# Gate products of the product-key experts: the first-index one-hots written to DRAM in one half and read back in the other

## The chip, the cores and the metric

The kernel runs on one core of one Trainium2 chip. The metric is the device time of one execution, in microseconds (us). Three runs of the kernel before gave 2181.5, 2175.8 and 2181.01 us, so its median is 2181.01 us.

## What is computed

The program is a decoder trunk of two layers over 256 positions of width 1024. Each layer has a mixer (four groups: differential attention, a convolution module, a gated convolution, a spatial gating unit) and then a product-key expert stage. Only the expert stage matters here:

```python
def peer_ffn(h, wq, keys, u_tab, v_tab):
    q = (h @ wq).reshape(b, s, PEER_HEADS, 2, PEER_HALF)
    sc = jnp.einsum('bshpd,hpnd->bshpn', q, keys)
    half_s, half_i = lax.top_k(sc, PEER_TOPK)                 # 16 of 128 keys, for each of two halves
    cand = half_s[..., 0, :, None] + half_s[..., 1, None, :]
    top_s, top_c = lax.top_k(cand.reshape(..., 256), PEER_TOPK)
    i1 = take(half_i[..., 0, :], top_c // 16)                 # first index, 0..127
    i2 = take(half_i[..., 1, :], top_c % 16)                  # second index, 0..127
    expert = i1 * 128 + i2                                    # one of 16384 single-neuron experts
    gate = jax.nn.softmax(top_s)
    act = gelu(einsum('td,thkd->thk', h, u_tab[expert]))
    return einsum('thk,thkd->td', gate * act, v_tab[expert])
```

Each of the 256 tokens picks 8 heads x 16 = 128 experts. The kernel gathers nothing: it computes the activation of all 16384 experts for all tokens, multiplies each by its gate (zero for experts not picked), and multiplies the result with the whole table v.

## The kernel before

**Stages.** In each layer, after `queries` and `topk`, two long loops stream the tables u and v through the TensorE. One step of either loop takes one 128x1024 fp32 block (512 KB) of the table. `Stream.load` (line 152) reads it into a raw tile (4 of them), `Stream.split` turns it into a rounded part `hi` (ScalarE, line 164) and a remainder `lo` (line 171, on GpSimd or on VectorE by a share: 0.8 of them on GpSimd in the stretches that matter here, 0.4 in the second half of `down`), with three buffers each, two steps ahead of use. All loads are issued by SyncE in one queue.

`up` has 128 steps, one for each value of the second index (the low part of the expert number is the partition). A step is 24 matmuls of 256 columns (lines 323 to 325) and a Gelu on ScalarE (line 845) into `acts`, four tiles of 32 steps each. `down` has 128 steps of 12 matmuls of 512 columns (line 874). A step needs the activations of its 128 experts split in two: `prep` makes the rounded part on ScalarE (line 860) and the remainder on VectorE (line 861, tile `mid`, two of them), one step ahead.

**The gates.** Between the two, `gates` scales the activations. For 8 tokens at a time (a block) it builds a one-hot of the first index, `o1` (128 picks x 8 tokens x 128 values, fp16, line 816, 128x1024), a one-hot of half of the second index, `o2` (128x512, line 819), and `og`, that one-hot times the gate, as two fp16 parts (two operations at line 823). Sixteen small matmuls (line 828) make the gate of every expert of that half for the 8 tokens in a PSUM bank. Two operations at line 834 multiply the bank into two tiles of `acts`; they are called the closing pair here. One half of the second index (`hf` 0, values 0 to 63) is done beside the second 64 steps of `up`, the other (`hf` 1, values 64 to 127) beside the first 64 steps of `down`, before the steps that use it. Each half is 32 blocks, made by two generators of 16 blocks each (even and odd blocks). `o1` does not depend on the half and is built in both, so line 816 runs 2 layers x 2 halves x 32 = 128 times.

**What sets the order.** `Background` interleaves such generators with the steps: each `yield` gives a VectorE cost, a latency and a TensorE cost, and after each step of `up` or `down` `pump(STEP)` lets as much background work in as the planned VectorE time allows, earlier generators first. `GATECOST` is (0.7, 1.2, 0.7, 0.9): `o1`, `o2` with `og`, the matmuls, the closing pair. A scheduler of the tile framework then sets the order on each engine, and may place an instruction some steps from where the code records it. After step 63 of `down` in layer 0 the same planner feeds in 40 operations of the modulation for layer 1 (line 247); the scheduler moves the first of them ahead into the steps with gates.

Of the kernel before, what the change touches and what calls it, by code (L numbers as in the profile page):

```python
# [12 lines left out]
FP16 = mybir.dt.float16  # L13
U32 = mybir.dt.uint32
AF = mybir.ActivationFunctionType
ALU = mybir.AluOpType
AX = mybir.AxisListType

P = 128
D = 1024  # L20
T = 256
# [18 lines left out]
GATECOST = (0.7, 1.2, 0.7, 0.9)  # L40
# [140 lines left out]
class Trunk:  # L181
# [618 lines left out]
            nc.vector.tensor_tensor(out=glo, in0=gv, in1=ghi, op=ALU.subtract)  # L800
            yield 1.2

    def gates(self, hf, acts, first):

        nc, one = self.nc, self.one
        half = self.iota[:, 64 * hf:64 * hf + 64]
        for t0 in range(8 * first, T, 16):  # L810
            o1 = one.tile([P, 4, P, 2], FP16, name="o1", bufs=2)
            o2 = one.tile([P, 4, 64, 2], FP16, name="o2", bufs=1)
            og = one.tile([P, 4, 2, 64, 2], FP16, name="og", bufs=2)
            i1, i2 = [self.idx[:, s, t0:t0 + 8].rearrange("p (a j) -> p a j", j=2) for s in range(2)]
            g = self.gidx[:, 2 * t0:2 * t0 + 16].rearrange("p (a j) -> p a j", j=2)
            nc.vector.tensor_tensor(out=o1, in0=self.iota[:, None].to_broadcast([P, 4, P, 2]),  # L816
                                    in1=i1[:, :, None].to_broadcast([P, 4, P, 2]), op=ALU.is_equal)
            yield GATECOST[0], 0.3
            nc.vector.tensor_tensor(out=o2, in0=half[:, None].to_broadcast([P, 4, 64, 2]),  # L819
                                    in1=i2[:, :, None].to_broadcast([P, 4, 64, 2]), op=ALU.is_equal)  # L820
            for s in range(2):
                gs = g.rearrange("p (a s) j -> p a s j", s=2)[:, :, s]
                nc.vector.tensor_tensor(out=og[:, :, s], in0=o2, in1=gs[:, :, None].to_broadcast([P, 4, 64, 2]), op=ALU.mult)  # L823
            yield GATECOST[1], 0.3
            b = self.accs(1)[0] if hf == 0 else self.bank()
            for j in range(8):
                for s in range(2):
                    nc.tensor.matmul(b[:, 64 * j:64 * j + 64], o1[:, j // 2, :, j % 2], og[:, j // 2, s, :, j % 2],  # L828
                                     start=s == 0, stop=s == 1)
            yield 0.0, 0.5, GATECOST[2]  # L830
            b = b.rearrange("p (j c) -> p c j", j=8)
            for s, act in enumerate(acts):
                a = act[:, :, t0:t0 + 8]
                nc.vector.scalar_tensor_tensor(out=a, in0=b[:, 32 * s:32 * s + 32], scalar=1.0 / GSCALE, in1=a,  # L834
                                               op0=ALU.mult, op1=ALU.mult)
            yield GATECOST[3]
# [48 lines left out]
    def experts(self, l, area):  # L885
        nc = self.nc
        sc, hb = self.queries(l, area)

        def picks():
            yield from self.topk(sc, area)  # L890
            if l + 1 < L:
                area.reset()
                cr = self.cond(area)
                bufs = [area.take(D + 1) for _ in range(4)]
                yield from self.mod_tiles(l, list(range(40, 48)), cr, bufs, pace=PACE[0])
                yield from self.mod_tiles(l + 1, list(range(8)), cr, bufs, pace=PACE[0])

        self.bg.add(picks())
        acts = [self.big(32, T) for _ in range(2)]
        self.stream.pool_share = SHARE[0]  # L900
        run = self.up(hb, acts)
        next(run)
        self.stream.pool_share = SHARE[1]
        acts += [self.big(32, T) for _ in range(2)]
        for i in range(2):
            self.bg.add(self.gates(0, acts[0:2], i))
        next(run)
        self.bg.finish()
        for i in range(2):
            self.bg.add(self.gates(1, acts[2:4], i))  # L910
        self.stream.pool_share = SHARE[2]
        run = self.down(acts)
        next(run)
        self.stream.pool_share = SHARE[3]
        self.m = Carve(self.big(), self.big())
        if l + 1 < L:
            cr = self.cond(self.m)
            bufs = [self.m.take(D + 1) for _ in range(4)]
            self.bg.add(self.mod_tiles(l + 1, list(range(8, 48)), cr, bufs, pace=PACE[1]))
            self.m.reset()  # L920
        next(run)
        self.bg.finish()
        self.m2 = Carve(self.big())
        if l + 1 < L:
            self.params(l + 1)
            self.bias = self.m.take(4, 256)
        y = self.m2.take(2, D)
        for tt in range(2):
            for d in range(2):
                eng = nc.vector.tensor_copy if d else nc.scalar.copy  # L930
                eng(out=y[:, tt, 512 * d:512 * d + 512], in_=self.acc[2 * tt + d])
        for c in range(NC):
            b = self.bank()
            for tt in range(2):
                nc.tensor.transpose(out=b[:, P * tt:P * tt + P], in_=y[:, tt, P * c:P * c + P], identity=self.ident)
            nc.vector.scalar_tensor_tensor(out=self.xT[:, c], in0=b[:, 0:T], scalar=self.modT[:, l, 40 + c:41 + c],
                                           in1=self.xT[:, c], op0=ALU.mult, op1=ALU.add)
            if l + 1 == L:
                self.last_stats(c, NC if c == NC - 1 else c - 2)
# [191 lines left out]
```

## Time and profile before

| | |
|---|---|
| median of three runs | 2181.01 us (2175.8 to 2181.5) |
| the profiled execution's own time | 2180.3 us |
| its span, first to last instruction | 2178.4 us |
| TensorE matmuls busy | 1932.3 us (89% of the span) |
| VectorE busy | 1673.4 us (77%) |
| GpSimd busy | 1277.4 us (59%) |
| ScalarE busy | 951.2 us (44%) |
| read from HBM | 371.9 MB, written 1.6 MB |

The profiled execution lies 0.7 us under the median; 1.9 us of it lie outside the span. In the profile PE is the TensorE's matmuls and PEld its weight loads, DVE is VectorE, ACT ScalarE, POOL GpSimd, SP SyncE. A line number is that of the kernel. Tile names are shown without their buffer numbers, so `o1` and `o2` are both `o`, told apart by their size. The arrow reads "out<-in". A trace answer for a stretch gives busy time inside it and the number of instructions; the granted clock of the TensorE is a share of full speed.

### The profile page before, as it was taken

Reading aid. Unit: us, or ns where it says so; the run is one execution under the profiler, and the core shown is the slowest. Engines: PE = TensorE matmul, PEld = TensorE weight load, DVE = VectorE, ACT = ScalarE, POOL = GpSimd, SP = SyncE. Lnnn points to the kernel's source line nnn. Section 1 sums busy time; section 2 is a strip of 40 time slices with the busy share of each in tenths; the row PEclk is TensorE's granted clock in tenths of the full one; section 3 lists DMA queues with packets and bytes.
Section 4 is the critical chain, followed back from the end, with each engine's and each line's share of the span. In section 5 each row is a group of like instructions: output and inputs, shape, how many; then the busy total and the mean of one; then the engine's idle time right before and its main releaser. Section 6 shows DMA issues by size and latency. Waiting matters only on the chain. (4 is left out here: it accounts for less than half of the span.)

```text
span 2178.4 us, 35318 instructions
## 1 busy us (share of the span) xinstructions
PE 1932.3 (89%) x13718; PEld 1736.7 (80%) x13718; DVE 1673.4 (77%) x2739; ACT 951.2 (44%) x1441; POOL 1277.4 (59%) x518
## 2 busy tenths in 40 slices
PE   4767997999999888899994889999999998889998
PEld 3667997998999666677874779999999976768886
DVE  6997699768892999987556676997598778884555
ACT  4344442443344333345552554444343443335554
POOL 6535676984566554543347657899565655545333
PEclk7888998999999998999997999999999999999999
DMA  7555445754455446687651444556444554446663
GB/s 263 197 187 175 159 161 186 249 175 136 141 169 175 136 130 210 248 283 264 194 184 58 136 136 140 182 164 186 153 156 152 168 155 130 138 132 191 194 193 116
DMA packets 104522, 375.82 MB, mean 173 GB/s; under 512 B 11900, under 2 KB 13217, under 8 KB 104098
## 3 DMA queue, kind: packets, MB, share of 16 engines
q1 hardware_dynamic: 104354, 373.57, 52.6%
q8 instruction: 107, 1.75, 0.3%
q14 instruction: 61, 0.50, 0.1%
HBM read 371.94 MB, written 1.58 MB: 171 GB/s over the span
## 5 line engine op out<-in xcount | busy, mean ns | idle before, releaser
L171 POOL TENSOR_TENSOR lo<-raw,hi 128x1024 fp32r<-128x1024 f32 x473 | 1234.4, 2617 | 858.2 <-ACT hi L164 836.0
L164 ACT ACTIVATE hi<-raw 128x1024 fp32r<-128x1024 f32 x600 | 635.5, 1060 | 643.7 <-issue 374.0
L325 PE MATMUL bank<-mid,lo 128*128 128x256 f32 x2432 | 700.8, 288 | 47.8 <-POOL lo L171 46.8
L323 PE MATMUL bank<-mid,hi 128*128 128x256 f32 x2432 | 707.9, 292 | 25.3 <-ACT hi L164 11.5
L324 PE MATMUL bank<-mid,hi 128*128 128x256 f32 x2432 | 700.1, 288 | 18.4 <-DVE mid L313 9.2
L874 PE MATMUL acc<-hi,mid 128*128 128x512 f32 x2048 | 585.8, 404 | 63.6 <-DVE mid L861 62.8
L325 PEld LDWEIGHTS bank<-mid,lo 128*128 128x128 f32 x2432 | 477.3, 196 | 52.3 <-POOL lo L171 51.1
L874 PEld LDWEIGHTS acc<-hi,mid 128*128 128x128 f32 x2048 | 390.9, 195 | 159.7 <-DVE mid L861 79.2
L323 PEld LDWEIGHTS bank<-mid,hi 128*128 128x128 f32 x2432 | 478.0, 197 | 31.2 <-ACT hi L164 13.5
L324 PEld LDWEIGHTS bank<-mid,hi 128*128 128x128 f32 x2432 | 478.1, 197 | 20.5 <-DVE mid L313 10.9
L861 DVE TENSOR_TENSOR mid<-big,mid 128x256 fp32r<-128x256 f32 x256 | 201.9, 793 | 197.1 <-PE acc L874 174.8
L874 PE MATMUL acc<-lo,mid 128*128 128x512 f32 x1024 | 327.1, 401 | 1.2 <-DVE lo L171 1.0
L860 ACT ACTIVATE mid<-big 128x256 fp32r<-128x256 f32 x256 | 107.0, 418 | 434.0 <-PE acc L874 426.4
L874 PEld LDWEIGHTS acc<-lo,mid 128*128 128x128 f32 x1024 | 198.0, 194 | 45.2 <-DVE lo L171 1.6
L171 DVE TENSOR_TENSOR lo<-raw,hi 128x1024 fp32r<-128x1024 f32 x127 | 159.5, 1256 | 82.1 <-ACT hi L164 81.3
L247 DVE SCALAR_TENSOR_TENSOR big<-big 128x1025 f32<-128x1025 f32 x96 | 175.3, 1841 | 17.5 <-DMA big<-wmod 17.5
L816 DVE TENSOR_TENSOR o<-iota,idx 128x1024 f16<-128x1024 f16 x128 | 187.0, 1462 | 0.0
L823 DVE TENSOR_TENSOR og<-o,gidx 128x512 f16<-128x512 f16 x256 | 181.7, 747 | 1.1
L819 DVE TENSOR_TENSOR o<-iota,idx 128x512 f16<-128x512 f16 x128 | 145.9, 1140 | 2.9
L828 PEld LDWEIGHTS <-o 128*128 128x128 f16 x2048 | 69.8, 99 | 41.3 <-issue 25.3
L845 ACT ACTIVATE big<-bank 128x256 f32<-128x256 f32 x256 | 93.5, 365 | 0.0
L834 DVE SCALAR_TENSOR_TENSOR big<-acc,big 128x256 f32<-128x256 f32 x128 | 47.8, 414 | 38.8 <-PE acc L828 38.8
(200 smaller groups left out, 1569.9 us busy)
## 6 DMA issues: line engine op xcount, KB each, us to landing
raw<-u SPq DMA_DIRECT2D x256, 512.0 KB, 3.5
raw<-v SPq DMA_DIRECT2D x256, 512.0 KB, 3.6
big<-wmod SPq DMA_DIRECT2D x96, 512.5 KB, 5.0
raw<-win SPq DMA_DIRECT2D x40, 512.0 KB, 3.5
raw<-wq SPq DMA_DIRECT2D x32, 512.0 KB, 3.5
raw<-wout SPq DMA_DIRECT2D x16, 512.0 KB, 3.5
big<-keys SPq DMA_DIRECT2D x2, 1024.0 KB, 6.1
xT<-xT SPq DMA_DIRECT2D x2, 512.0 KB, 4.3
```

Source lines behind the costliest of these rows:

```text
L164: nc.scalar.activation(out=hi, in_=raw, func=AF.Copy)
L171: eng.tensor_tensor(out=lo, in0=raw, in1=hi.bitcast(F32), op=ALU.subtract)
L247: nc.vector.scalar_tensor_tensor(out=w, in0=w, scalar=1.0, in1=sc, op0=ALU.mult, op1=ALU.mult, accum_out=self.modT[:, l, j:j + 1])
L323: mm(out, whi, hhi, start=start, stop=False)
L324: mm(out, whi, hlo, start=False, stop=False)
L325: mm(out, wlo, hhi, start=False, stop=stop)
L816: nc.vector.tensor_tensor(out=o1, in0=self.iota[:, None].to_broadcast([P, 4, P, 2]), in1=i1[:, :, None].to_broadcast([P, 4, P, 2]), op=ALU ...
L819: nc.vector.tensor_tensor(out=o2, in0=half[:, None].to_broadcast([P, 4, 64, 2]), in1=i2[:, :, None].to_broadcast([P, 4, 64, 2]), op=ALU.is ...
L823: nc.vector.tensor_tensor(out=og[:, :, s], in0=o2, in1=gs[:, :, None].to_broadcast([P, 4, 64, 2]), op=ALU.mult)
L860: nc.scalar.activation(out=a[:, 0], in_=src, func=AF.Copy)
L861: nc.vector.tensor_tensor(out=a[:, 1], in0=src, in1=a[:, 0].bitcast(F32), op=ALU.subtract)
L874: nc.tensor.matmul(self.acc[2 * tt + d], a[:, s, P * tt:P * tt + P], w[:, 512 * d:512 * d + 512], start=i == 0 and s == 0 and w is whi, st ...
```

## The change

The one-hots `o1` of half 0 are written to DRAM tiles (`kept`, 32 for each layer, 256 KB each) as they are made. In half 1 they are not built again. Each is read back: the first one when its generator starts, the next one as soon as the matmuls of the present block are recorded. `o1` has three buffers where it had two. Since half 1 has no operation at line 816, its `yield` (0.7 planned VectorE cost and 0.3 latency) is not passed there either.

```diff
-    def gates(self, hf, acts, first):
+    def gates(self, hf, acts, first, kept):
         nc, one = self.nc, self.one
         half = self.iota[:, 64 * hf:64 * hf + 64]
+        def onehot(t0):
+            return one.tile([P, 4, P, 2], FP16, name="o1", bufs=3)
+
+        def fetch(t0):
+            o1 = onehot(t0)
+            nc.sync.dma_start(out=o1, in_=kept[t0 // 8])
+            return o1
+
+        o1 = fetch(8 * first) if hf else None
         for t0 in range(8 * first, T, 16):
-            o1 = one.tile([P, 4, P, 2], FP16, name="o1", bufs=2)
+            if not hf:
+                o1 = onehot(t0)
             o2 = one.tile([P, 4, 64, 2], FP16, name="o2", bufs=1)
             og = one.tile([P, 4, 2, 64, 2], FP16, name="og", bufs=2)
...
-            nc.vector.tensor_tensor(out=o1, in0=self.iota[:, None].to_broadcast([P, 4, P, 2]),
-                                    in1=i1[:, :, None].to_broadcast([P, 4, P, 2]), op=ALU.is_equal)
-            yield GATECOST[0], 0.3
+            if not hf:
+                nc.vector.tensor_tensor(out=o1, in0=self.iota[:, None].to_broadcast([P, 4, P, 2]),
+                                        in1=i1[:, :, None].to_broadcast([P, 4, P, 2]), op=ALU.is_equal)
+                nc.sync.dma_start(out=kept[t0 // 8], in_=o1)
+                yield GATECOST[0], 0.3
...
                     nc.tensor.matmul(b[:, 64 * j:64 * j + 64], o1[:, j // 2, :, j % 2], og[:, j // 2, s, :, j % 2],
                                      start=s == 0, stop=s == 1)
+            if hf and t0 + 16 < T:
+                o1 = fetch(t0 + 16)
             yield 0.0, 0.5, GATECOST[2]
...
+        kept = [self.dram.tile([P, 4, P, 2], FP16, name=f"kept{l}_{i}") for i in range(T // 8)]
         for i in range(2):
-            self.bg.add(self.gates(0, acts[0:2], i))
+            self.bg.add(self.gates(0, acts[0:2], i, kept))
         next(run)
         self.bg.finish()
         for i in range(2):
-            self.bg.add(self.gates(1, acts[2:4], i))
+            self.bg.add(self.gates(1, acts[2:4], i, kept))
```

The change moves instructions as well. The first place is VectorE in the first steps of `down` in layer 0 (tiles `o_`: 128x1024 is `o1`, 128x512 is `o2`; `mid` is `prep` for one step). Before, three blocks come in four steps, and the two blocks of a pair share a step:

```order
L816 TENSOR_TENSOR o_7506<-iota,idx 128x1024
L861 TENSOR_TENSOR mid<-big,mid 128x256
L819 TENSOR_TENSOR o_7507<-iota,idx 128x512
L823 TENSOR_TENSOR og<-o_7507,gidx 128x4x128 x2
L819 TENSOR_TENSOR o_7511<-iota,idx 128x512
L861 TENSOR_TENSOR mid<-big,mid 128x256
L834 SCALAR_TENSOR_TENSOR big<-bank,big 128x32x8 x2
L816 TENSOR_TENSOR o_7510<-iota,idx 128x1024
L823 TENSOR_TENSOR og<-o_7511,gidx 128x4x128 x2
L819 TENSOR_TENSOR o_7580<-iota,idx 128x512
```

The same place with the change (line 831 is `o2`, 835 `og`, 848 the closing pair, 875 `prep`):

```order
L831 TENSOR_TENSOR o_7651<-iota,idx 128x512
L875 TENSOR_TENSOR mid<-big,mid 128x256
L848 SCALAR_TENSOR_TENSOR big<-bank,big 128x32x8 x2
L835 TENSOR_TENSOR og<-o_7651,gidx 128x4x128 x2
L171 TENSOR_TENSOR lo<-raw,hi 128x1024
L831 TENSOR_TENSOR o_7697<-iota,idx 128x512
L875 TENSOR_TENSOR mid<-big,mid 128x256
L848 SCALAR_TENSOR_TENSOR big<-bank,big 128x32x8 x2
L835 TENSOR_TENSOR og<-o_7697,gidx 128x4x128 x2
```

With the change there is exactly one block to one step, and `og` of the next block stands behind the closing pair of the block before. On the TensorE (no rows of it stand here; its order gives the counts) the 32 blocks of half 1 then end after step 33 of `down` in both layers (12 matmuls between one block and the next), where they ended after step 49 in layer 0 and after step 54 in layer 1.

The second place is SyncE's queue at the start of `down` in layer 0. Before, it holds nothing but table blocks there:

```order
L152 DMA raw<-u 128x1024 x85
L152 DMA raw<-v 128x1024 x36
```

With the change (`kept_` the DRAM tile of a block, line 815 the read):

```order
L815 DMA o_7412<-kept_0_4441 128x1024
L152 DMA raw<-u 128x1024 x2
L815 DMA o_7419<-kept_1_4442 128x1024
L152 DMA raw<-u 128x1024 x2
L815 DMA o_7463<-kept_2_4443 128x1024
L152 DMA raw<-u 128x1024 x9
L152 DMA raw<-v 128x1024 x8
L815 DMA o_7509<-kept_4_4445 128x1024
L152 DMA raw<-v 128x1024
L815 DMA o_7555<-kept_6_4447 128x1024
```

From there on a read and a table block alternate until block 31. The even blocks come first (0, 2, ... 30), then the odd ones; block 1, read at the start, keeps its buffer until the even ones are done, so these share the two others. The read that stands behind table block v[m+5] is for the matmuls behind step m+1.

## Rows read from the trace of the kernel before

**Rows 1.** Busy time of the engines in three stretches; the first row names the columns.

```profile
core 0: us, PE busy (x) PEld busy (x) DVE busy (x) ACT busy (x) POOL busy (x), PEclk, DMA share, GB/s
697.60:829.10 131.50, 113.83 (x772) 89.89 (x771) 120.72 (x176) 50.10 (x70) 62.98 (x26) 0.94 0.44 140
1542.40:1752.60 210.20, 202.13 (x2027) 200.37 (x2025) 169.62 (x204) 83.10 (x127) 125.53 (x51) 0.98 0.50 158
1752.70:1961.45 208.75, 181.47 (x1151) 142.11 (x1151) 177.75 (x248) 80.67 (x112) 107.89 (x44) 0.93 0.43 137
```

**Rows 2.** The same, line 874 alone: length, PE, PEld, clock, DMA share, GB/s.

```profile
697.60:953.00 255.40, 202.17 (x769) 151.62 (x770) 0.93 0.56 190
906.20:953.00 46.80, 43.05 (x181) 33.38 (x182) 1.00 0.78 275
1752.70:1961.45 208.75, 170.17 (x648) 127.28 (x649) 0.93 0.43 137
1961.45:2162.80 201.35, 201.34 (x888) 166.57 (x888) 1.00 0.59 181
```

**Rows 3.** Groups, 1752.7 to 1961.45 us: busy us, mean ns | idle before, releaser.

```profile
L861 DVE TENSOR_TENSOR mid<-big,mid 128x256 fp32r<-128x256 f32 x56 | 46.5, 841 | 37.7 <-PE acc L874 28.0 <-ACT mid L860 9.6
L823 DVE TENSOR_TENSOR og<-o,gidx 128x512 f16<-128x512 f16 x60 | 42.6, 744 | 0.2
L816 DVE TENSOR_TENSOR o<-iota,idx 128x1024 f16<-128x1024 f16 x30 | 33.8, 1128 | 0.0
L819 DVE TENSOR_TENSOR o<-iota,idx 128x512 f16<-128x512 f16 x29 | 29.2, 1009 | 0.7
L834 DVE SCALAR_TENSOR_TENSOR big<-bank,big 128x256 f32<-128x256 f32 x62 | 23.1, 413 | 0.0
L171 DVE TENSOR_TENSOR lo<-raw,hi 128x1024 fp32r<-128x1024 f32 x11 | 13.4, 1219 | 1.9 <-ACT hi L164 1.9
...
L171 POOL TENSOR_TENSOR lo<-raw,hi 128x1024 fp32r<-128x1024 f32 x44 | 110.6, 2514 | 101.3 <-ACT hi L164 100.1 <-DVE mid L861 0.7 <-DVE o L819 0.3
```

**Rows 4.** Shortest, median and longest duration in ns: line 816, then line 861 (layer 1).

```profile
L816 DVE TENSOR_TENSOR o<-iota,idx x128: 672/683/2923, 445.5 to 1949.5; 128x1024 f16<-128x1024 f16 x128
...
L861 DVE TENSOR_TENSOR mid<-big,mid x56: 410/425/2627, 1752.8 to 1961.2; 128x256 fp32r<-128x256 f32 x56
```

**Rows 5.** Time line around one stall (columns: start us, duration us, engine, line).

```profile
1849.98 0.75 DVE L823 TENSOR_TENSOR og<-o,gidx 128x512 f16<-128x512 f16 x2
1850.32 2.61 POOL L171 TENSOR_TENSOR lo<-raw,hi 128x1024 fp32r<-128x1024 f32 x1 [0.81 <-ACT hi L164]
1850.76 2.45 DVE L819 TENSOR_TENSOR o<-iota,idx 128x512 f16<-128x512 f16 x1
...
1855.85 0.43 DVE L819 TENSOR_TENSOR o<-iota,idx 128x512 f16<-128x512 f16 x1
...
1853.60 1.46 PE L874 MATMUL acc<-hi,mid 128*128 128x512 f32 x4 [3.00 <-DVE mid L861]
...
1855.71 1.91 PE L874 MATMUL acc<-hi,mid 128*128 128x512 f32 x4
```

**Rows 6.** Waits of 1752.7 to 1961.45 us (total us, times, longest us).

```profile
PE acc L874 <- DVE mid L861: 27.2, 13, 3.8
```

**Rows 7.** Time line of the PE behind a shorter stall.

```profile
1787.86 1.19 PE L874 MATMUL acc<-hi,mid 128*128 128x512 f32 x4 [1.88 <-DVE mid L861]
...
1789.34 1.07 PE L874 MATMUL acc<-hi,mid 128*128 128x512 f32 x4
...
1792.52 0.66 PE L828 MATMUL bank<-og,o 128*128 128x64 f16 x16
```

**Rows 8.** Transfers: KB each and median us from issue to landing.

```profile
raw<-v SPq DMA_DIRECT2D x256, 512.0 KB, 3.6
...
out<-big SPq DMA_DIRECT2D x4, 256.0 KB, 2.8
...
big<-sguw SPq DMA_DIRECT2D x2, 256.0 KB, 6.0
```

## The prediction

> **What bounds the kernel now.** I read first which stretches hold line 816. It runs beside the second half of `up` and beside the first 64 steps of `down`, and only the second kind loses it. The stretch 1752.7 to 1961.45 us is layer 1's share of `down` with gates: 648 matmuls at 12 a step are 54 steps in 208.75 us [rows 2]. The stretch behind it, without gates, has 888 matmuls in 201.35 us, so 74 steps at 2.72 us [rows 2]. At that pace, and with 0.66 us [rows 7] for the 16 small matmuls of each of the 32 blocks, 54 steps would need 168 us. So some 41 us of this stretch are lost.
>
> Next, who is late. The TensorE's matmuls wait for VectorE's `mid` 13 times, 27.2 us in all [rows 6]. Some more goes to the slow matmuls behind such stalls, below. VectorE is busy 177.75 of 208.75 us there (85%), and in layer 0's first 33 steps 120.72 of 131.50 us (92%) [rows 1]. VectorE sets the pace.
>
> Then what VectorE does. `o1` takes 0.68 us undisturbed but up to 2.92 us, `prep` 0.41 us but up to 2.63 us [rows 4]. The time line shows why: GpSimd's subtraction starts at 1850.32 and takes 2.61 us; `o2` starts at 1850.76 and ends with it, after 2.45 us where it takes 0.43 us alone, and `og`, 0.75 us a pair, had run just ahead [rows 5]. The closing pair is not touched: 62 operations have a mean of 413 ns [rows 3]. Behind such a pile-up the TensorE stands 3.00 us, and its next matmuls run at half rate, four of them in 1.91 us [rows 5]. Where it stood 1.88 us they did not: four in 1.07 us [rows 7]. The granted clock of the stretch is 0.93 in the mean [rows 2], mostly 2.4 GHz with some time at 1.2 GHz.
>
> **The change, part by part.** *Removed from VectorE:* 32 operations of line 816 in each layer. Their busy time in layer 1 is 33.8 us for the 30 in the stretch [rows 3], of which 30 x 0.68 = 20.4 us is their own and 13.4 us waiting for GpSimd. GpSimd's operations stay, and its wait falls on whatever comes next, so I credit only the 0.68 us. The Trainium skill, "SBUF — State Buffer", section "Who interferes with whom", gives the rule: a VectorE operation with two SBUF inputs and a GpSimd operation that reads SBUF exclude each other, and the later one is blocked to the end. By the row's whole busy time 32 operations would return 36 us a layer, by the rule 22 us; the trace bears the rule out, since `o2` at 1850.76 is held just as `o1` is.
>
> *The new pace.* With the change one block goes with each step, and all 32 end after step 33. I price a step by VectorE. The waits for GpSimd in layer 1 are what the lines took beyond their own times [rows 3 to 5]: `prep` 46.5 - 56 x 0.41 = 23.5, `og` 42.6 - 60 x 0.375 = 20.1, `o1` 13.4, `o2` 29.2 - 29 x 0.43 = 16.7, together 73.7 us over GpSimd's 44 operations, 1.68 us each. A step then costs `prep` 0.41, a fifth of a `lo` at 1.22 (0.24) and 0.8 GpSimd operations at 1.68 (1.34), 2.0 us. A block costs `o1` 0.68, `o2` 0.43, `og` 0.75, closing pair 0.83, 2.69 us; without `o1`, 2.01 us. This gives 54 x 2.0 + 32 x 2.69 = 194 us for the 208.75 us seen, 7.5% too little. In layer 0's 33 steps with 23 blocks (by the order) it gives 128 of 131.50 us, 2.5% too little. With one block a step it gives 4.0 us, and 4.1 to 4.3 us with these two surcharges. I take **4.2 us for each of the 33 steps**, 138.6 us. Bounds: if GpSimd's wait fell beside other work altogether, the TensorE would set the pace at 2.72 + 0.66 = 3.4 us; if each of its operations cost VectorE all of its 2.51 us, 0.41 + 0.24 + 2.01 + 2.01 = 4.67 us.
>
> *Layer 1:* 138.6 us, and 21 steps freed of gates at 2.72 us, 57.1 us, make 195.7 us where 208.75 us stand: **13.0 us gained**. *Layer 0* is compared over its first 64 steps, 255.40 us [rows 2], because modulation work fills the freed steps. Its steps without gates but with modulation took 46.80 us for 15, 3.12 us each [rows 2]. So 138.6 + 31 x 3.12 = 235.3 us, and 2 us for a few modulation operations that now come later: 237.3 us, **18.1 us gained**.
>
> *Added in `down`:* 32 reads of 256 KB a layer on SyncE's queue. A read starts when the matmuls of two blocks earlier are done, and is needed after the next step's twelve matmuls, 4.2 + 2.72 = 6.9 us later. A 512 KB block lands in 3.6 us, 256 KB to DRAM in 2.8 us; the longest, 6.0 us, was a 256 KB load queued behind others [rows 8]. I take it as hidden, under the step; if the step fell to 3.4 us, 6.1 us would be left, just enough. A table block queued behind a waiting read cannot start before a `lo` of the same step anyway. The volume rises from 137 GB/s at a DMA share of 0.43 [rows 1] to some 180 GB/s, less than the 275 GB/s seen at 906 us [rows 2].
>
> *Added in `up`:* 32 writes of 256 KB a layer, each waiting on SyncE for VectorE's `o1`, with table loads queued behind it. ScalarE and with it the TensorE would notice if a load came late. The cover is the four raw tiles, some steps of lead. If that were used up, the TensorE would wait: it is busy 202.13 of 210.20 us there [rows 1], so today's idle 8 us a layer is the nearest measure of what late VectorE work costs. I take 1 us a layer, 8 us as the upper end; the third buffer could also return some of the 8 us, so the lower end is a gain of as much.
>
> **Sum:** 13.0 + 18.1 - 2 = 29 us. The profiled execution took 2180.3 us, so **2151 us**; the median of the runs is 0.7 us above that execution.
>
> **The rivals.**
> *The TensorE takes over the pace.* At 3.4 us a step the 33 steps take 112.2 us; layer 1 gains 39.4, layer 0 44.5 us: about 2098 us. For it: a steady step has no pairs of blocks to pile up. Against it: GpSimd still works 2.0 us of each step. Chance 0.10.
>
> *GpSimd's wait falls on the path each time.* With one generator at work, closing pair, `og` and the next small matmuls form one chain through VectorE, and `og` comes just when GpSimd starts, as at 1849.98 and 1850.32 [rows 5]. At 4.67 us a step, 154.1 us, layer 1 loses 2.4 and layer 0 gains 2.6 us: with the 2 us of `up` 2182 us, no change. Chance 0.15.
>
> *The clock falls.* If standing 1 to 1.5 us in each step lowered the clock, twelve matmuls would take 5.4 us instead of 2.72. With half of the 33 steps so, at 6.1 us, the mean is 5.15 us: 170 us, 18 us lost in layer 1 and 13 us in layer 0, about **2214 us, slower**. For it: the slow matmuls behind the 3.00 us stall [rows 5]. Against it: none behind the 1.88 us stall [rows 7]. The Trainium skill, "TensorE: Matmul & The Clock Gate", Part 1, says that the throttled clock is the default and activity releases it; it names no share of activity that I could set against a step that is three quarters busy. Chance 0.08.
>
> *The reads come late.* The reading side sets the step once landing takes longer than step + 2.72 us, and makes it slower than before from 4.67 + 2.72 = 7.4 us on. At 8 us the step is 5.3 us, 175 us: 23 and 18 us lost, about 2224 us. For it: 6.0 us of a load behind others [rows 8]. Against it: 3.6 us for twice the size in the running queue. Chance 0.05.
>
> **How the numbers follow.** The forecast has the remaining 0.62, with steps of 3.8 to 4.5 us. At 3.8 us the gain is 26 + 31 - 2 = 55 us, about 2125 us, and the range goes 3 us below it for `up`: 2122 us. Upwards it takes in the chain of GpSimd's wait at 2182 us and the upper end for `up`, to 2188 us. That leaves out most of the fast rival (0.07) and the two slow ones (0.13), 2 in 10. A change of under 0.3%, 6.5 us, cannot be told from none here. Faster: the forecast, the fast rival and a small part of the chain's case, 0.72. Same: most of that case, 0.12. Slower: the two slow rivals and the rest of it, 0.16.
>
> **What would show it.** Right: line 816's successor runs 64 times; in `down` 33 steps of about 4.2 us, each with a pause of about 1 us before the small matmuls or before `mid`; steps of 2.72 us from there in layer 1; clock over 0.93; mean `o2`, `og` and `prep` no shorter than before; reads landing under 6 us with no wait of line 840 for them. Wrong: waits of the TensorE for a transfer into `o`, steps of over 4.7 us, half-rate matmuls in every second step, or a second half of `up` longer by more than 8 us.

## The result, and the profile after

The change takes **2121.01 us** (median of 4 runs, 2120.13 to 2122.38) where the kernel before took 2178.41 us in the same comparison (4 runs, 2175.54 to 2181.5): a ratio of 0.9739, 95% interval 0.9725 to 0.9753. It is faster, by 57 us. The forecast was a gain of 29 us, to 2151 us, with 2122 us as the lower end, 1 us above what was measured. The sign was right, but only about half of the gain was forecast.

The first part of the page after, busy us and share of the span of 2119.3 us:

```profile
PE 1913.8 (90%) x13718; PEld 1720.2 (81%) x13718; DVE 1613.3 (76%) x2675; ACT 953.4 (45%) x1441; POOL 1283.2 (61%) x518
```

Of the 59.1 us between the spans of the two profiles most is in the first 64 steps of `down`. They stand here for layer 0 and layer 1, first of the kernel before, with the columns of [rows 1]:

```profile
697.70:952.90 255.20, 215.65 (x1270) 167.55 (x1271) 242.46 (x318) 96.74 (x132) 128.16 (x52) 0.93 0.56 190
1752.80:1988.75 235.95, 208.75 (x1270) 164.72 (x1271) 189.39 (x261) 94.92 (x130) 126.50 (x52) 0.94 0.45 142
```

Of the change: the 33 steps with gates of each layer, the same 64 steps, and the 64 steps behind them in layer 1.

```profile
695.10:820.54 125.44, 114.69 (x898) 88.29 (x898) 119.52 (x192) 50.10 (x69) 62.53 (x26) 1.00 0.65 206
1720.80:1845.13 124.33, 114.88 (x899) 88.55 (x899) 120.73 (x191) 50.37 (x69) 65.35 (x28) 1.00 0.64 202
695.10:924.10 229.00, 205.38 (x1271) 158.01 (x1272) 217.38 (x282) 97.06 (x132) 133.03 (x52) 0.99 0.71 238
1720.80:1929.50 208.70, 199.25 (x1270) 158.44 (x1271) 158.81 (x231) 95.18 (x130) 124.18 (x52) 1.00 0.63 197
1929.50:2103.40 173.90, 173.90 (x769) 143.97 (x768) 88.67 (x101) 93.89 (x127) 61.18 (x26) 1.00 0.60 181
```

Layer 0 gained 26.2 us there and layer 1 27.2 us, 53.4 us together. A step with a block takes 125.44 / 33 = 3.80 and 124.33 / 33 = 3.77 us; 4.2 us was forecast. VectorE (third busy column) is busy 97% of the second row. The TensorE's own busy time over the 64 steps fell from 215.65 + 208.75 to 205.38 + 199.25 us, by 19.8 us, though it does the same matmuls: the granted clock went from 0.93 and 0.94 to 0.99 and 1.00. Pauses of the TensorE (over 1 us from the start of one matmul to that of the next) in these 128 steps went from 26 with 69.7 us in all to 22 with 27.8 us.

The groups of the change in the 33 steps of layer 1 (busy us, mean ns | idle before), which answer to [rows 3]:

```profile
L171 POOL TENSOR_TENSOR lo<-raw,hi 128x1024 fp32r<-128x1024 f32 x28 | 69.9, 2497 | 59.4 <-ACT hi L164 58.7 <-DVE o L831 0.7
L835 DVE TENSOR_TENSOR og<-o,gidx 128x512 f16<-128x512 f16 x60 | 63.4, 1097 | 0.0
L848 DVE SCALAR_TENSOR_TENSOR big<-bank,big 128x256 f32<-128x256 f32 x61 | 22.8, 416 | 0.0
L875 DVE TENSOR_TENSOR mid<-big,mid 128x256 fp32r<-128x256 f32 x34 | 19.4, 571 | 12.3 <-ACT mid L874 9.6 <-PE acc L888 2.6
L831 DVE TENSOR_TENSOR o<-iota,idx 128x512 f16<-128x512 f16 x29 | 14.5, 500 | 0.9
L171 DVE TENSOR_TENSOR lo<-raw,hi 128x1024 fp32r<-128x1024 f32 x7 | 8.5, 1219 | 0.0
```

The wait for GpSimd has moved onto `og`: its mean went from 744 to 1097 ns, while `o2` and `prep` came down from 1009 and 841 to 500 and 571 ns [rows 3]. The amount for each GpSimd operation has hardly changed. Beyond their own times the three took 63.4 - 60 x 0.375 = 40.9, 14.5 - 29 x 0.43 = 2.0 and 19.4 - 34 x 0.41 = 5.5 us, together 48.4 us over GpSimd's 28 operations: 1.73 us each, where 1.68 us was worked out of the kernel before.

The reads: count and durations of the issue (ns), and the time to landing (us); then all that the TensorE's matmuls wait for in the 33 steps of layer 1.

```profile
L815 SPq DMA_DIRECT2D o<-kept x64: 326/327/1238, 639.4 to 1834.0; - x64
...
DMA to landing us min/median/max: 2.7/3.6/5.3
...
PE bank L840 <- DVE og L835: 8.2, 13, 1.0
```

In the whole program 0.8 us of waiting is put down to the reads.

### The profile page after: what moved, and what is told of

Its sections match the earlier page's. It is cut to its first block, busy times and chain, and to the rows that moved or that the text cites. A ratio compares the mean times of both kernels' runs of the same rounds, so it can differ in the third digit from the quotient of the medians.

```text
span 2119.3 us, 35499 instructions
## 1 busy us (share of the span) xinstructions
PE 1913.8 (90%) x13718; PEld 1720.2 (81%) x13718; DVE 1613.3 (76%) x2675; ACT 953.4 (45%) x1441; POOL 1283.2 (61%) x518
## 3 DMA queue, kind: packets, MB, share of 16 engines
q1 hardware_dynamic: 122786, 407.13, 59.1%
## 5 line engine op out<-in xcount | busy, mean ns | idle before, releaser
L323 PE MATMUL bank<-mid,hi 128*128 128x256 f32 x2432 | 706.4, 291 | 23.2 <-ACT hi L164 12.6
L888 PE MATMUL acc<-hi,mid 128*128 128x512 f32 x2048 | 569.0, 394 | 18.8 <-DVE mid L875 18.4
L888 PEld LDWEIGHTS acc<-hi,mid 128*128 128x128 f32 x2048 | 378.4, 188 | 104.5 <-DVE mid L875 29.2
L875 DVE TENSOR_TENSOR mid<-big,mid 128x256 fp32r<-128x256 f32 x256 | 214.9, 842 | 190.3 <-PE acc L888 168.4
L888 PE MATMUL acc<-lo,mid 128*128 128x512 f32 x1024 | 317.5, 391 | 1.2 <-POOL lo L171 1.0
L835 DVE TENSOR_TENSOR og<-o,gidx 128x512 f16<-128x512 f16 x256 | 255.1, 1036 | 0.5
L888 PEld LDWEIGHTS acc<-lo,mid 128*128 128x128 f32 x1024 | 192.3, 188 | 43.0 <-POOL lo L171 1.4
L831 DVE TENSOR_TENSOR o<-iota,idx 128x512 f16<-128x512 f16 x128 | 106.5, 832 | 2.6
L827 DVE TENSOR_TENSOR o<-iota,idx 128x1024 f16<-128x1024 f16 x64 | 81.5, 1290 | 0.0
L414 DVE SCALAR_TENSOR_TENSOR big<-big,cols 128x256 f32<-128x256 f32 x128 | 75.9, 656 | 0.5
```

The lines of the kernel that those rows point to most:

```text
L323: mm(out, whi, hhi, start=start, stop=False)
L875: nc.vector.tensor_tensor(out=a[:, 1], in0=src, in1=a[:, 0].bitcast(F32), op=ALU.subtract)
L888: nc.tensor.matmul(self.acc[2 * tt + d], a[:, s, P * tt:P * tt + P], w[:, 512 * d:512 * d + 512], start=i == 0 and s == 0 and w is whi, st ...
```

## The experiments

The theory after the result: VectorE paces the steps with gates; the 0.68 us that `o1` takes there come back in full, and the even pace adds something, perhaps because long pauses and the half clock behind them go (no run tests that reason by itself). The rivals: the pace does it all; the third buffer or the transfers matter; GpSimd's share matters more than any of these.

| kernel | median us | ratio to before, 95% | 64 steps of `down`, layer 0 / 1, us | clock there |
|---|---|---|---|---|
| before | 2178.4 | 1 | 255.2 / 236.0 | 0.93 / 0.94 |
| the change | 2121.0 | 0.9739 (0.9725 to 0.9753) | 229.0 / 208.7 | 0.99 / 1.00 |
| before, even pace, 3 buffers | 2170.4 | 0.9964 (0.9952 to 0.9976) | 248.2 / 231.6 | 0.97 / 0.95 |
| change, old pace | 2131.7 | 0.9794 (0.9773 to 0.9815) | 238.5 / 211.6 | 0.94 / 0.98 |
| before, 3 buffers | 2179.3 | 1.0008 (0.9995 to 1.0021) | 252.8 / 234.8 | 0.92 / 0.95 |
| change, no transfers | 2126.5 | 0.9764 (0.9741 to 0.9787) | 227.0 / 209.5 | 0.99 / 1.00 |
| change, 2 buffers | 2129.4 | 0.9789 (0.9756 to 0.9822) | 230.8 / 210.0 | 0.99 / 1.00 |
| change, no GpSimd | 2073.3 | 0.9535 (0.9500 to 0.9570) | 198.4 / 192.9 | 1.00 / 1.00 |
| change, spread | 2117.5 | 0.9718 (0.9683 to 0.9753) | 229.6 / 203.0 | 0.96 / 1.00 |
| change, spread, no GpSimd | 2069.0 | 0.9503 (0.9474 to 0.9532) | 193.0 / 192.9 | 1.00 / 1.00 |
| before, no GpSimd | 2080.3 | 0.9549 (0.9523 to 0.9574) | 193.7 / 192.6 | 1.00 / 1.00 |
| before, spread, no GpSimd | 2082.9 | 0.9566 (0.9543 to 0.9590) | 193.2 / 193.0 | 1.00 / 1.00 |
| before, no GpSimd, 3 buffers | 2076.0 | 0.9528 (0.9509 to 0.9547) | 194.1 / 192.6 | 1.00 / 1.00 |
| change, spread, no GpSimd, again | 2066.8 | 0.9488 (0.9465 to 0.9512) | 192.9 / 192.9 | 1.00 / 1.00 |

**The pace alone.** Against the kernel before, with three buffers as well:

```diff
-            yield GATECOST[0], 0.3
+            if not hf:
+                yield GATECOST[0], 0.3
```

> Half 1 builds o1 on VectorE as before, but without its yield and with three buffers: the order of the TensorE is that of the change, one block to each step of down, done after step 33, and nothing goes to DRAM. Theory 1 (the gain is the 0.68 us that leave VectorE for each block; a steady pace only spares the long pauses): a VectorE step of 2.0 + 2.69 = 4.7 us, 33 steps 155 us in each layer where the change took 124 to 125 us and before 131 us; layer 1 then about 3 us slower and layer 0 about 4 us faster than before, and with some 7 us from up a total of 2165 to 2180 us, at a clock near 1.0 in those steps. Rival 2 (the gain is the pace; the work of o1 fits beside the rest): steps of 3.8 to 4.0 us, total 2120 to 2135 us.

The total fell into theory 1's span, in part by luck: layer 1 was 4.4 us faster where 3 us slower was expected, and the 7 us counted for `up` did not come (843.4 us for its 256 steps, 840.4 before). The 64 steps, layer 0 and 1, then the 33 steps:

```profile
700.75:948.90 248.15, 209.51 (x1270) 162.00 (x1271) 232.89 (x311) 96.77 (x132) 133.47 (x52) 0.97 0.57 189
1753.50:1985.10 231.60, 206.70 (x1270) 164.81 (x1271) 174.37 (x260) 94.89 (x130) 126.69 (x52) 0.95 0.47 144
700.75:844.72 143.97, 118.87 (x899) 92.10 (x899) 136.23 (x221) 50.01 (x69) 67.04 (x26) 0.95 0.41 129
1753.50:1900.73 147.23, 122.33 (x899) 94.91 (x899) 138.37 (x222) 49.46 (x69) 67.54 (x27) 0.92 0.38 119
```

The 33 steps took 144.0 and 147.2 us, 4.36 and 4.46 us each, not 4.7: here too the step formula is too high. With the reads instead of `o1` the same order of the TensorE gives 3.80 and 3.77 us, so one `o1` costs 0.56 and 0.69 us of a step. Theory 1's clock near 1.0 in those steps did not come: it was 0.95 and 0.92. Pauses of over 2.6 us fell from 16 to 4 in the 128 steps, but all pauses of over 1 us took 74.8 us where they took 69.7.

**The reads alone, at the old pace.** Against the change, the yield is passed in both halves:

```diff
-                yield GATECOST[0], 0.3
+            yield GATECOST[0], 0.3
```

> The change, but half 1 keeps the yield of 0.7 planned cost: the reads replace o1, and the order of the TensorE is that before (three blocks in four steps, pairs in one step, done after step 49 and 54). Theory 1 (removal of VectorE time): a mean VectorE step of 2.0 + 0.75 x 2.01 = 3.5 us in the first 33 steps, some 120 us, and about 3.1 us in the steps behind them with a block in every second one: 64 steps in about 200 to 205 us where the change took some 209 us in layer 1; total 2105 to 2125 us. Rival 2 (the pace): pairs of blocks still hold mid back by 2.7 us and more, half-rate matmuls follow, clock 0.93 to 0.95 in the gate steps, total 2145 to 2165 us.

2131.7 us lies between the two spans. The 64 steps:

```profile
687.85:926.30 238.45, 210.43 (x1270) 164.63 (x1271) 212.77 (x280) 97.17 (x132) 129.65 (x52) 0.94 0.67 227
1724.80:1936.40 211.60, 200.33 (x1270) 159.74 (x1271) 168.13 (x231) 94.94 (x130) 126.28 (x52) 0.98 0.60 194
```

In layer 1 the 33 steps took 120.0 us and the 31 behind them 2.96 us each, about as theory 1 had them; its own parts, 120 and 31 x 3.1, add up to 216 us and not to 200 to 205. Against the kernel with three buffers the reads, with the writes that they need, return 0.0214 of the time of before at the old pace (1.0008 - 0.9794; of 2180 us, 46.7 us), and the pace alone 0.0044, 9.6 us; both together 0.0269, 58.6 us. The two parts nearly add up. Not all of the 46.7 us is `o1`: in the profiles the 64 steps of `down` became shorter by 14.3 us in layer 0 and 23.2 us in layer 1, 0.45 and 0.72 us for one `o1`, and `up`, which builds as many as before, by 10.5 us.

**The third buffer alone.** `name="o1", bufs=3` in the kernel before.

> The kernel before with three buffers of o1 and nothing else. If the some 7 us that the change gained outside the steps with gates in down come from the third buffer in up, the total is 2170 to 2173 us and the time from the end of down in layer 0 to its start in layer 1 falls by about 4 us. Rival: the buffer does nothing there and those 7 us are something else: 2176 to 2181 us.

Nothing in the total: the rival was right. A saving in `up` is not to be had from the buffer alone, though the next run shows that the buffer shifts time inside `up`.

**No transfers.** The kernel writes nothing to DRAM and leaves the one-hots of half 1 out: each generator of half 1 sets one tile to ones, once.

```diff
-            nc.sync.dma_start(out=o1, in_=kept[t0 // 8])
+            nc.vector.memset(o1, 1.0)
...
-                nc.sync.dma_start(out=kept[t0 // 8], in_=o1)
...
-            if hf and t0 + 16 < T:
-                o1 = fetch(t0 + 16)
```

> The change without its transfers: nothing is written to DRAM, and in half 1 each generator uses one tile of ones for all its blocks, set once, so the gates of half 1 are left out of the computation in all but form. Order and VectorE work of the steps are those of the change. Theory 1 (reads and writes are hidden): 2117 to 2124 us, steps of 3.7 to 3.8 us. Rival 3 (the transfers take something, by SyncE's queue in up or by traffic in down): 2105 to 2116 us, with the difference in the stretch of up or in the 33 steps.

The steps of `down` are those of the change (227.0 and 209.5 us), so reads and traffic cost nothing there. The total is not lower but some 5 us higher, above both spans. The intervals of the two kernels overlap, but the traces show where the time is. Taken from the starts of its matmuls, `up` lasted in one profile each (us, layer 0 / 1):

| kernel | first 64 steps | second 64 steps | all 256 |
|---|---|---|---|
| before (2 buffers, no writes) | 216.7 / 192.3 | 217.4 / 214.0 | 840.4 |
| before, 3 buffers | 221.2 / 196.5 | 214.6 / 208.6 | 841.0 |
| change, no transfers (3 buffers, no writes) | 221.1 / 196.4 | 214.6 / 208.6 | 840.7 |
| change, 2 buffers | 215.0 / 192.3 | 215.7 / 212.6 | 835.6 |
| the change (3 buffers, writes) | 216.3 / 191.6 | 214.1 / 208.6 | 830.6 |

The other runs fall in with these: 840.8 to 843.4 us without writes, 829.1 to 833.0 us with writes and three buffers. So the third buffer shortens the second half and, without writes, lengthens the first by as much; with writes only the saving is left. Near the end of the first half the time lines of the change with and without writes differ. Without writes, the TensorE stands 4.47 us for a copy of the top-k stage (lines 795 and 796) that VectorE reaches late, behind operations held by GpSimd:

```profile
1496.17 2.95 DVE L834 TENSOR_TENSOR og<-o,gidx 128x512 f16<-128x512 f16 x2
1499.16 2.46 DVE L830 TENSOR_TENSOR o<-iota,idx 128x512 f16<-128x512 f16 x1
1501.93 0.28 DVE L796 TENSOR_SCALAR big<-bank 128x128 f32<-128x128 f32 x1
...
1502.36 0.55 PE L323 MATMUL bank<-mid,hi 128*128 128x256 f32 x1 [4.47 <-DVE big L796]
```

With them, a table load stands in SyncE's queue behind a write, comes late, and leaves GpSimd idle for 3.14 us. VectorE passes in that gap, its pair of `og` in 0.76 us:

```profile
1486.85 0.33 SPq L829 DMA_DIRECT2D kept<-o  x1
1487.27 2.17 SPq L152 DMA_DIRECT2D raw<-u  x4
...
1491.08 1.06 ACT L164 ACTIVATE hi<-raw 128x1024 fp32r<-128x1024 f32 x1 [4.35 <-DMA raw<-u]
...
1490.19 0.76 DVE L835 TENSOR_TENSOR og<-o,gidx 128x512 f16<-128x512 f16 x2
1491.33 0.48 DVE L795 CAST idx<-bank 128x128 f16<-128x128 f32 x2
...
1492.22 11.89 POOL L171 TENSOR_TENSOR lo<-raw,hi 128x1024 fp32r<-128x1024 f32 x5 [3.14 <-ACT hi L164]
```

The trace of the kernel before with three buffers, layer 1, has the same stall:

```profile
PE bank L323 <- DVE big L796: 4.5, 1, 4.5
```

It is 4.5 us in both layers of all four runs with three buffers and no writes, and 1.6 us in both layers of all three with two buffers and no writes. With writes it is gone, but for 1.6 us in one layer with two buffers. So it is no chance of one run. That the delayed load is what spares the stall is read from two time lines; no run moved that load by itself.

**Two buffers.** `bufs=2` in the change.

> The change with two buffers of o1 instead of three. Block 1, read at the start, holds one until the even blocks are done, so a read of the next even block must wait for the matmuls of the present one. The reads took 3.6 us (median) to land in the change, so one period of the first 16 steps is 3.6 us of landing, 0.66 us of small matmuls and the issue, some 4.6 to 5.5 us instead of 3.8. Theory (the reads are hidden by the buffer alone): the TensorE's loads or matmuls of the gates wait for the transfer in most of these 16 steps, 13 to 27 us lost in each layer, total 2145 to 2175 us. Rival (VectorE paces the steps and a read lands in time even so): 2119 to 2128 us, no waits for o.

The time came out near the rival's span, 1 us above it, but the waits of the first theory came (the TensorE for the reads, in the 33 steps of layer 0, then of layer 1):

```profile
PE bank L840 <- DMA o<-kept: 9.9, 10, 3.9
...
PE bank L840 <- DMA o<-kept: 7.1, 10, 1.7
```

Yet the 64 steps took only 1.8 and 1.3 us longer. The wait for `og` fell from 7.9 to 4.0 us and from 8.2 to 4.2 us in exchange; in layer 0 the 33 steps still took 7.5 us longer, and the 31 behind them 5.7 us less. Of the 8 us that the median lost 5 us are in `up`, by the table above.

**No GpSimd in these steps.** The third number of `SHARE`, 0.8, is 0 in the change:

```diff
-SHARE = (1.0, 0.8, 0.8, 0.4)
+SHARE = (1.0, 0.8, 0.0, 0.4)
```

> The change, with every remainder lo on VectorE in the first 64 steps of down (a share of 0 for GpSimd instead of 0.8). Theory A (each GpSimd operation holds VectorE for 1.7 us, all of it in VectorE's time): a step is 0.41 + 1.22 + 2.01 = 3.64 us, no operation of VectorE is stretched (og 0.375, o2 0.43, prep 0.41 us in the mean), the 33 steps take 120 us instead of 124 to 125, total 2109 to 2119 us. Rival B (half or more of that waiting lies beside other work): VectorE has 0.98 us more to do in each step, steps of 4.2 to 4.7 us, 14 to 30 us lost in each layer, total 2145 to 2180 us.

2073 us, 48 us under the change, far more than either theory had. Groups of VectorE in the 33 steps of layer 1, then the 64 steps of both layers:

```profile
L171 DVE TENSOR_TENSOR lo<-raw,hi 128x1024 fp32r<-128x1024 f32 x33 | 40.2, 1219 | 1.2 <-ACT hi L164 1.2
L848 DVE SCALAR_TENSOR_TENSOR big<-bank,big 128x256 f32<-128x256 f32 x62 | 23.4, 419 | 0.0
L835 DVE TENSOR_TENSOR og<-o,gidx 128x512 f16<-128x512 f16 x60 | 22.7, 419 | 0.0
L875 DVE TENSOR_TENSOR mid<-big,mid 128x256 fp32r<-128x256 f32 x35 | 14.9, 426 | 14.8 <-ACT mid L874 12.5 <-PE acc L888 2.3
L831 DVE TENSOR_TENSOR o<-iota,idx 128x512 f16<-128x512 f16 x29 | 12.3, 423 | 0.4
```

```profile
1688.24:1796.70 108.46, 108.46 (x899) 86.84 (x899) 104.41 (x219) 49.53 (x69) 0.23 (x1) 1.00 0.71 232
...
694.75:893.15 198.40, 195.13 (x1270) 156.07 (x1271) 177.21 (x331) 96.89 (x132) 0.19 (x1) 1.00 0.81 272
1688.25:1881.10 192.85, 192.85 (x1270) 156.75 (x1271) 156.00 (x282) 94.92 (x130) 0.22 (x1) 1.00 0.66 215
```

No operation is stretched any more. A step takes 108.46 / 33 = 3.29 us, and the TensorE is busy in all of it: it sets the pace now. A `lo` costs VectorE 1.22 us; the same `lo` on GpSimd had cost it 1.73 us of waiting. For 28 of them that is 14 us, about the 15.9 us by which these 33 steps became shorter. The Trainium skill, "GPSIMD Engine Reference", "4.1 Engine selection", sends elementwise work on tiles to VectorE because GpSimd takes about twice as long for two inputs. The rows agree, 2497 against 1219 ns, but that alone would not show here, since in these steps of the change no wait of the TensorE is put down to GpSimd; what decides is the wait that it causes.

The lines above also show one reason why the formula was too high. Their busy times add up to 113.5 us, yet VectorE was busy 104.41 us: its operations overlap at their ends in the records. The time line of this run has three in a row, each starting before the one ahead of it has ended (1740.62 + 0.76 = 1741.38; 1741.29 + 0.75 = 1742.04):

```profile
1740.62 0.76 DVE L848 SCALAR_TENSOR_TENSOR big<-bank,big 128x256 f32<-128x256 f32 x2
1741.29 0.75 DVE L835 TENSOR_TENSOR og<-o,gidx 128x512 f16<-128x512 f16 x2
1741.96 1.22 DVE L171 TENSOR_TENSOR lo<-raw,hi 128x1024 fp32r<-128x1024 f32 x1
```

**Spread.** In the change, `yield GATECOST[3] + (2.0 if hf else 0.0)` at the end of a block.

> The change with 2.0 more of planned VectorE cost behind each closing pair of half 1: one block to a step still, but in 3 steps of 5, done after step 56 in layer 0 and some steps later than 42 in layer 1. Theory A (steps without a block are bound by the TensorE at 2.72 us and have VectorE time to spare, which the spread uses): with prep one step ahead VectorE evens out, and 64 steps cost the TensorE's 64 x 2.72 + 32 x 0.66 = 195 us and a few pauses, 196 to 204 us instead of 208.7 in layer 1, less in layer 0 where the modulation fills VectorE: total 2098 to 2114 us. Rival B (a step with a block stands alone, 3.77 us, and one without gives nothing back): 33 x 3.77 + 31 x 2.72 = 208.7 us as before, 2117 to 2126 us. Rival C (uneven steps bring pauses of 2.3 us and more and half-rate matmuls back): 2126 to 2145 us.

The total lies in rival B's span, but as the sum of two effects: theory A in layer 1, and in layer 0 the lower clock of rival C:

```profile
695.10:924.70 229.60, 207.43 (x1270) 159.40 (x1271) 212.25 (x280) 96.79 (x132) 130.58 (x52) 0.96 0.69 234
1723.40:1926.40 203.00, 197.73 (x1270) 155.21 (x1271) 169.18 (x231) 94.87 (x130) 125.35 (x52) 1.00 0.61 202
```

Layer 1 gained 5.7 us. In layer 0, where the modulation fills VectorE, the clock fell to 0.96 and nothing was gained. The median differs from the change by less than the intervals.

**Spread, no GpSimd.** Both edits.

> Both at once: the spread blocks and every lo on VectorE in the first 64 steps of down. VectorE then has 0.41 + 1.22 = 1.63 us for a step and 2.01 us for a block, 1.63 + 0.6 x 2.01 = 2.8 us in the mean, under the TensorE's 2.72 + 0.6 x 0.66 = 3.1 us. Theory A of both: 64 steps in 195 to 200 us in layer 1, total 2095 to 2112 us, no stretched operation and clock 1.00. Rivals: as with the two parts alone, 2117 us and more.

193.0 and 192.9 us, all of them TensorE. That is theory A's mechanism, with more gained than it gave: its 64 steps began at 195 us, and 2069 us lies 26 us under its span.

**Is the change needed for that?** The share of 0 in the kernel before, with no other edit; then also the even order of the spread run (the yield behind `o1` left out in half 1, 2.0 more behind the closing pair).

> The kernel before, with every lo on VectorE in the first 64 steps of down (share 0 for GpSimd) and nothing else: no transfers, o1 built twice, the order of the TensorE nearly that before. From the run of the change without GpSimd VectorE needs 1.6 us for a step and about 1.6 us for a block; o1 adds 0.6 to 0.7 us to a block. Theory A (GpSimd's share is the larger cost, and most of what the reads returned would come back without them): 54 steps with 32 blocks need 54 x 1.6 + 32 x 2.25 = 158 us of VectorE and 165 us of the TensorE, with pauses for the pairs some 170 to 185 us where 208.7 stood, total 2100 to 2130 us. Rival B (without the reads VectorE stays the bound at one and a half times that): 2140 us and more.

> The same with the even order of the TensorE of the spread change (no yield behind o1 in half 1, 2.0 more of planned cost behind the closing pair), o1 built on VectorE, nothing sent to DRAM. Theory A (once no step is bound by VectorE, building o1 again costs nothing): 3 blocks in 5 steps need VectorE 1.6 + 0.6 x 2.25 = 2.95 us a step, the TensorE 2.72 + 0.6 x 0.57 = 3.06 us, so 64 steps in 193 to 200 us in layer 1 and total 2069 to 2085 us, as with the reads. Rival B (o1 stays on the path, 0.7 us for each block as in the runs at GpSimd's share of 0.8): 45 us over the spread change without GpSimd, 2105 to 2120 us.

One number in the kernel before gives 2080 us, 20 us better than theory A's best end and 41 us better than the change. Its 64 steps:

```profile
698.00:891.65 193.65, 193.63 (x1271) 156.90 (x1272) 184.25 (x348) 97.19 (x132) 0.20 (x1) 1.00 0.68 223
1696.75:1889.30 192.55, 192.54 (x1271) 157.17 (x1272) 170.87 (x312) 95.02 (x130) 0.24 (x1) 1.00 0.55 176
```

Both runs take as long in `down` as the spread change without GpSimd, though VectorE builds 64 more `o1`. Where the TensorE is busy all the time, `o1` is free. Spreading gave nothing more here; the second run came as its theory A had it.

**What the transfers are still worth.** The kernel before with the share of 0 and three buffers, beside the spread change without GpSimd once more.

> The kernel before with every lo of the first 64 steps of down on VectorE and three buffers of o1, still nothing sent to DRAM. The kernel before with the share alone took 2080 us, and its steps of down are as short as with the reads; what is left to the change without GpSimd lies in the second half of up (211.6 us a layer against 203 to 208). Theory A (the third buffer returns it): 2070 to 2076 us. Rival B (the buffer does nothing there, as it did nothing to the kernel before): 2078 to 2084 us, and the rest belongs to the writes and where they put the table loads.

> The change with the spread blocks and no GpSimd in these steps once more, beside the run above on the same chip: 2063 to 2071 us. If the DRAM transfers are worth nothing once VectorE is not the bound, it is no more than 0.3% (6 us) faster than the kernel above; if they are, 9 us or more.

9 us remain between them (the intervals just touch), hardly any of it in `down` (386.6 against 385.8 us). It is in `up`: in the profiles its first 64 steps took 221.2 and 196.4 us without writes (layer 0 and 1) and 214.8 and 192.5 us with them, the second 64 214.7 and 208.6 us against 213.8 and 208.6. The stall of 4.5 us described above is in both layers of the one and in neither of the other. The median of 2076 us lies at the edge of theory A; whether the third buffer returns the 4 us between 2076 and 2080 us stays open, since the intervals overlap and `up` took 840.8 and 842.0 us in the two profiles. The fastest kernel of the study is the spread change without GpSimd, 2067 to 2069 us.

## Why the prediction was right and wrong

*What bounds the kernel:* right in saying that VectorE paced these steps. It stopped one question short. GpSimd's operations cost VectorE 73.7 us of waiting in layer 1's stretch by the prediction's own working, more than three times the 22 us of `o1` that it credits, and the run with the share of 0 in the kernel before, 98 us faster, shows that this was the larger lever.

*0.68 us for each `o1`, not its whole busy time:* right in layer 1, somewhat high in layer 0. 22 us a layer were credited by the rule of exclusion, 36 us by busy time. With the same pace on both sides the 64 steps of layer 1 returned 23.2 us (old pace) and 22.9 us (even pace), those of layer 0 14.3 and 19.2 us. The Trainium skill's rule ("SBUF — State Buffer", "Who interferes with whom") is that of a VectorE operation with two SBUF inputs and a GpSimd operation that reads SBUF the later one is blocked. The trace agrees: the wait stayed, 1.68 and then 1.73 us for each GpSimd operation, and fell on other operations.

*4.2 us for each step:* **this is the step that failed.** It measured 3.80 and 3.77 us. With 3.77 us in the same sum, layer 1 gives 33 x 3.77 + 57.1 = 181.5 us, 27.2 us gained, which is what was measured. The price had a formula (4.0 us) and a surcharge of 2.5 to 7.5%, 0.2 us, taken from the kernel before. The formula counted a block for each of the 33 steps, where the rows have some 30 and give 128.6 / 33 = 3.90 us. It summed busy times by line, which overlap: the lines add up to 128.6 us and VectorE was busy 120.7 us, 0.24 us a step less. The surcharge stood for VectorE's idle time beside pauses and half-rate matmuls (31 of 208.75 us before [rows 1]). With one block to a step VectorE was idle 3.6 us in 33 steps, 0.11 us a step. So 4.2, less 0.10, 0.24 and 0.20, plus 0.11, is 3.77. In the kernel before the two errors had nearly hidden each other: the formula's 194 us are 16 us more than VectorE's 177.75 busy us, and the idle 31 us are not in it.

*The steps behind the gates:* 2.72 us in layer 1, (208.70 - 124.33) / 31, as forecast. In layer 0 (229.00 - 125.44) / 31 = 3.34 us where 3.12 us was taken, so its gain was 26.2 and not the 31 us that a step of 3.80 us would have given.

*The transfers:* right. The longest read took 5.3 us, and leaving all transfers out shortened no step. The 6.0 us taken as the longest landing was not the longest in the trace before, where three loads of 64 KB of constants took 6.7 us in the median; nothing hung on it. In `up` the sign was wrong: a loss of 1 us a layer was priced, and in the profiles `up` gained 9.8 us, of which 4 us were lost again elsewhere. Neither the buffer (841.0 us) nor the writes with two buffers (835.6 us) explain it alone; both together do (830.6 us, 840.4 before). The prediction had allowed for a gain there of up to 8 us, by the third buffer, but took only 3 us of it into the range; with 8 us its lower end would have been 2115 us.

*The sum:* of the 30 us between the forecast gain and the 59.1 us of the profiles, the step of 3.80 and 3.77 us makes 27 us, `up` and what lies around it 8 us, and layer 0 behind the gates 5 us the other way.

*Rivals:* no clock loss, and no late reads. That the TensorE takes over the pace was given 0.10 and did not come with this change, but is what the share of 0 brings, at 3.29 us where 3.4 us was priced. The argument against it ("GpSimd still works 2.0 us of each step") named what stood in the way. That GpSimd's wait would fall on `og` was right, but not its price: a pause of up to 1.0 us, not a step of 4.67 us (13 waits, 8.2 us in all, in layer 1).

*What would show it:* 64 operations, 2.72 us, reads under 6 us and a clock over 0.93 came. That mean `og`, `o2` and `prep` would each be no shorter did not: the wait gathered on `og`, and only its sum stayed.

## What to carry to other kernels

Before taking work off the engine that sets the pace, ask who makes it wait: an offloaded operation that blocks it for longer than it would take itself (1.73 against 1.22 us here) is no help, and one number can be worth more than a rewrite. A cost that is summed by lines has to be checked against the engine's busy time, and idle time found beside pauses must not be carried over to an order that has none. An operation that was worth 0.7 us on the path is worth nothing once another engine is the bound, so such gains do not add.

## What was not expected of the hardware

- The clock's share. In the 128 steps the same matmuls took 19.8 us more of busy time before than after. Even pacing alone took back 8.2 us of that (209.51 + 206.70 us), though in its own 33 steps the clock, 0.95 and 0.92, was as low as in the same steps before (0.94 and 0.92); the reads alone 13.6 us (210.43 + 200.33 us in the old-pace run); both all of it. The pause of 1 to 1.5 us in each step that the prediction feared did not come: 22 pauses of over 1 us in 128 steps.
- VectorE's operations overlap at their ends in the records, by 0.08 and 0.09 us in the three shown; over a step this was 0.24 us in the change and (113.5 - 104.41) / 33 = 0.28 us without GpSimd.
- Reads of 256 KB from DRAM landed in 3.6 us in the median, the same as table blocks of 512 KB [rows 8] in the same queue.
